# A rebuilt S5 layer with a halved carry pass, weight tiles 320 bytes further on, and stationary values in latent attention

## The chip, the core and the metric

The kernel runs on one core of a Trainium2 chip. The metric is the device time of one execution in microseconds (us), lower being better. The core's engines, each with an instruction queue of its own, are PE (matrix products, TensorE), DVE (VectorE), ACT (ScalarE), POOL (GpSimd) and SP (SyncE, which here issues most DMA transfers). An engine takes its instructions strictly in order: one that waits holds up all behind it.

## What is computed

A network of four layers on 256 positions of 1024 features, all in fp32. The first layer is a state space mixer (S5), the second block attention, the third and fourth are a mixer of three branches (latent attention, convolution, retention) with a feed-forward part. Two pieces matter here.

```python
def s5_mixer(h, w_in, ...):
    u, z = split(h @ w_in)                       # 2 x 1024 columns, u in 64 groups of 16
    # per group and each of 64 complex states: s[t] = a * s[t-1] + f * (b @ u[t])
    _, _, s_re, s_im = lax.associative_scan(_complex_linear_combine, ...)
    y = gelu(c_re @ s_re - c_im @ s_im + d_skip * u)
    y = y * sigmoid(y @ w_glu + b_glu) * silu(z)
    return y @ w_out

def mla_branch(c_q, c_kv, k_pe, ...):            # 8 heads, 96 for scores, 64 for values
    s = q_nope @ k_nope + q_pe @ k_pe
    p = softmax(s * scale)
    return (p @ v) @ w_o
```

## The kernel before

**Products of the later layers.** fp32 products are made of three products of a reduced form: each weight tile is loaded as raw (`wtile`, line 142; DMA L149 on SP), ACT copies its high part hi (L158), DVE subtracts it for the low part lo (L160), and `mm3` (L163) issues L165, L166 and L167. There the activations (xTh, xTl) are the stationary operand, and hi or lo is streamed, 512 columns at a time. `wbuf` (L135) deals out the buffers in turn, in stage 2 (all behind the S5 layer) six of them: of each six tiles four come from the pool wp and two from the pool sp.

```python
        pool, bufs = (self.wp, 4) if i % (4 + more) < 4 else (self.sp, more)
```

Where an sp tile lies follows from the tiles made before it in that pool, one of them the attention mask (`consts2`, L323). By the built program's addresses, the four hi and lo buffers of sp begin at 64 bytes past a multiple of 128 (190016, 194112, 198208, 202304), all those of wp on a multiple of 128. `gemm` (L169) calls `pump` after each tile, which takes one piece of small work from a list (`fill2`); so attention is woven into the weight products.

**The S5 layer** (`s5`, L598). ACT squares x and sums (L625), DVE finds 1/rms (`rsqrt`, L628 and L120 to 133), ACT and DVE scale x (L630, L631), PE turns it (L637), ACT applies the gain (L639). PE then makes u in two halves h of 512 columns (L428, four weight tiles each, two accumulators of two 128-column blocks); `ev_u` stores each block to memory (L649, L650), and four loads per half bring it back regrouped as U (L692). Meanwhile DVE works out the layer's parameters (`s5_params`, `s5_w`, `s5_c`), and PE turns the input matrices into W (L586).

Then for q = 0, 1 PE forms W times U (L729), ACT copies the result into X (L734). X holds 4 chunks g of 16 steps, 32 pairs of groups, real and imaginary. Between q = 0 and q = 1 stands `taps` (L696): products L703, a copy K (L707), the addition of the skip (L708), a store (L709) and 16 loads of M (L716).

DVE scans the 15 steps inside all chunks at once (L743 two products, L745, L747). The carry pass takes g = 1, 2, 3 in turn: powers Q times the carry (L754, four of 128x512), two sums (L756), the next carry (L758) and the additions to X (L762). PE meanwhile makes z (L428) and the part of y inside the chunks (`inside`, L768, L775; `see` copies L779), then waits for X and adds the rest of y (L796, half 0, one z tile, half 1). ACT copies Y (L807), SP stores it (L811) and loads it regrouped (L814), ACT applies gelu (L817), and the gated products follow (L454 to L456).

**Latent attention** (`mla`, L1022) puts 17 pieces into `fill2`. `score(h)`: two products of 256 columns (L1072), DVE's maximum (L1074) and its negative (L1075), two exponentials on ACT with their sums (L1078). `value(h)`: four transposes (L1088), ACT's copy pT (L1090), four products of pT with 64 columns of v streamed (L1097), into a tile with a position per partition. `out(g)` for four heads: reciprocals of the sums, a product of 128x512 on DVE (L1104), four transposes (L1110) and the split into hi and lo.

The order of instructions on an engine is that in which the program issues them, except where small pieces are interleaved with products when it is built, so the built order is read below.

Of the kernel before, what the change touches and what calls it, by code (L numbers as in the profile page):

```python
# [9 lines left out]
F32 = mybir.dt.float32  # L10
# [40 lines left out]
class Net:  # L51
# [267 lines left out]
    def consts2(self):  # L319
# [3 lines left out]
        self.mask = self.sp.tile([128, 128], F32, tag="mask", name="mask", bufs=1)  # L323
# [137 lines left out]
    def s5_params(self):  # L461
# [27 lines left out]
        yield lambda: nc.scalar.activation(cs, r, AF.Sin)  # L489
# [4 lines left out]
        tt(pw[:, 1:3, :, 1], cs, mag[:, None, :].to_broadcast([128, 2, 32]), op=ALU.mult)  # L494
# [4 lines left out]
        def times(out, a, n, re, im):  # L499

            sh = [128, 2, 32, n]
            m = [self.sp.tile(sh, F32, tag="s5m%d" % n, name=self.nm("s5m"), bufs=2) for _ in range(2)]
# [31 lines left out]
        nc.scalar.activation(self.Q[:, :, 0, :], pw[:, :, :, 4], AF.Copy)  # L534
# [54 lines left out]
    def s5_c(self, cab, q, after):  # L589
# [3 lines left out]
        for i in range(2):  # L593
            with self.tc.issue_after(after.ins):
# [3 lines left out]
    def s5(self, x_in):  # L598
# [23 lines left out]
        xr = [self.page([128, 1024], "s5xr") for _ in range(2)]  # L622
        r = self.tmp([128, 2], "pn_r")
        for t in range(2):
            nc.scalar.activation(xr[t], x[t], AF.Square, scale=1.0 / 32, accum_out=r[:, t:t + 1])  # L625
        params = self.s5_params()
        sincos = next(params)
# [5 lines left out]
        for b in range(0, 8, 2):  # L633
            pt = self.small()
            for i in range(2):
                for t in range(2):
                    nc.tensor.transpose(pt[:, i * 256 + t * 128:i * 256 + t * 128 + 128], xr[t][:, (b + i) * 128:(b + i + 1) * 128], self.ident)  # L637
            for i in range(2):
                last = nc.scalar.activation(hT[(b + i) // 4][:, (b + i) % 4], pt[:, i * 256:(i + 1) * 256], AF.Identity, scale=g0[:, b + i:b + i + 1])  # L639
            if b == 0:  # L640
                with self.tc.issue_after(last.ins):
                    sincos()
# [28 lines left out]
        for q in range(4):  # L671
            self.s5_c(cab, q, last)
# [14 lines left out]
        for h in range(2):  # L687
            for go in self.gemm_raw(xs, 512, lambda b, p, h=h: ev_u(4 * h + b, p)):
                go()
            for t in range(4):  # L690
                r = h * 64 + (3 - t) * 16
                self.load_after = nc.sync.dma_start(U[r:r + 16].rearrange("p a g j -> p (a g) j"), uv[h, t])  # L692
# [3 lines left out]
        def taps():  # L696
# [11 lines left out]
            tt(K[:, :, 0:16], K[:, :, 0:16], dk, op=ALU.add)  # L708
            nc.scalar.dma_start(kv[:, :, 48:112], K)  # L709
            M = [self.page([128, 8, 2, 64], "s5M") for _ in range(2)]  # L710
            km = kd.rearrange("(q m c) n -> q c m n", q=2, c=16)
            for q in range(2):
                for t in range(4):
                    r = q * 64 + (3 - t) * 16
                    for h in range(2):
                        nc.sync.dma_start(M[h][r:r + 16].rearrange("p a g n -> p (a g) n"), km[q][:, 16 * h:16 * h + 16, 48 - 16 * t:112 - 16 * t])  # L716
            return M

# [3 lines left out]
        for q in range(2):  # L722
# [12 lines left out]
            if q == 0:  # L735
                M = taps()

        for k in range(1, 16):
# [8 lines left out]
            tt(xo, pr[:, :, :, 0:32], xo, op=ALU.add)  # L747
        for g in range(1, 4):
# [700 lines left out]
```

## Time and profile before

| | us |
|---|---|
| median of 3 runs | 1262.59 (1262.33 to 1263.01) |
| the profiled execution | 1260.24 |
| its span | 1258.5 |
| PE, DVE, ACT busy in the span | 1217.2, 918.9, 663.6 |
| S5 stage: first product, scan, carry pass, Y | 15.00, 59.60, 85.65, 107.25 |

The span is the time from the first to the last record of the profile; 1.74 us of the execution lie around it. Instructions are named by line and engine, operands by the program's tile names with their numbers left out, and "out<-in" gives what is written and read. In a timeline the first number is the start from the beginning of the span, the second the time from the start of the first to the end of the last of the merged instructions, and "x4" their count; a note in brackets is the idle time ahead of them and who ended it. A product of fp32 operands shows as two records, and a record is longer than the distance to the next, since products are pipelined.

### The profile page before, as it was taken

What the parts mean: (1) busy time and instruction counts of PE and PEld (TensorE: products, weight loads), DVE (VectorE), ACT (ScalarE), POOL (GpSimd) and SP (SyncE); (2) the same over time, 40 slices, a digit from 0 to 9 for tenths busy, and PEclk for the clock granted to TensorE, in tenths of its full rate; (3) what the DMA queues carried; (4) which work ended last, traced back from release to release, by engine and by line L of the source; (5) the groups of instructions that cost most, each with busy time, mean ns of one, the idle gap of its engine ahead of it and who ended that gap; (6) DMA issues with size and microseconds to landing.
All of it is one profiled execution on the core that took longest, in us unless ns stands there. A gap on an engine that the chain in (4) does not pass through costs nothing.

```text
span 1258.5 us, 17821 instructions
## 1 busy us (share of the span) xinstructions
PE 1217.2 (97%) x6516; PEld 1013.5 (81%) x6516; DVE 918.9 (73%) x1871; ACT 663.6 (53%) x1107; POOL 3.6 (0%) x16
## 2 busy tenths in 40 slices
PE   6988899999999999999999999999999999999997
PEld 5877787788888888887888887888888887888886
DVE  6793789786899998856655545899997856655544
ACT  5412676766665545546544535666545446544431
POOL 0000000000000000000000000000000000000000
PEclk9998999999999999999999999999999999999999
DMA  8744566542744545563765663644544564765661
GB/s 312 131 68 116 187 195 201 166 142 81 226 136 143 166 144 167 169 213 102 240 193 153 203 231 106 210 137 148 167 150 154 181 200 119 235 185 158 203 208 49
DMA packets 125368, 210.60 MB, mean 167 GB/s; under 512 B 22112, under 2 KB 31328, under 8 KB 125280
## 3 DMA queue, kind: packets, MB, share of 16 engines
q1 hardware_dynamic: 121344, 205.29, 53.7%
q10 hardware_dynamic: 3936, 4.18, 1.1%
q8 instruction: 51, 0.84, 0.3%
q14 instruction: 37, 0.30, 0.1%
HBM read 205.83 MB, written 3.60 MB: 166 GB/s over the span
## 4 chain that ended last, share of the span: by engine, by line
PE 82%; DVE 9%; ACT 3%; DMA 2%; issue 2%; SPq 1%; DVEq 0%; ACTq 0%
PE mm L165 23%; PE mm L167 23%; PE mm L166 23%; PE mm L428 2%; DVE lo L160 2%; PE sm L203 2%; ACT hi L158 1%; PE sm L1097 1%; PE sm L1189 1%; DVE cacc L935 1%; PE sm L1072 1%; DVE s5pr L743 1%; DVE s5fx L754 1%; PE sm L796 1%; PE sm L1177 1%
## 5 line engine op out<-in xcount | busy, mean ns | idle before, releaser
L160 DVE TENSOR_TENSOR lo<-raw,hi 128x1024 fp32r<-128x1024 f32 (+2 forms) x372 | 440.9, 1189 | 230.3 <-ACT hi L158 228.7
L158 ACT ACTIVATE hi<-raw 128x1024 fp32r<-128x1024 f32 (+2 forms) x372 | 382.1, 1032 | 364.9 <-PE mm L167 286.1
L165 PE MATMUL mm<-hi,xTh 128*128 128x512 f32 (+2 forms) x1152 | 451.1, 394 | 1.7 <-ACT xTh L193 1.5
L167 PE MATMUL mm<-hi,xTl 128*128 128x512 f32 (+2 forms) x1152 | 443.7, 386 | 0.3
L166 PE MATMUL mm<-lo,xTh 128*128 128x512 f32 (+2 forms) x1152 | 443.4, 385 | 0.1
L165 PEld LDWEIGHTS mm<-hi,xTh 128*128 128x128 f32 x1152 | 216.4, 188 | 48.9 <-ACT xTh L193 7.2
L167 PEld LDWEIGHTS mm<-hi,xTl 128*128 128x128 f32 x1152 | 216.3, 188 | 46.1 <-DVE t L297 1.5
L166 PEld LDWEIGHTS mm<-lo,xTh 128*128 128x128 f32 x1152 | 216.6, 188 | 41.2 <-DVE lo L160 0.5
L935 DVE SCALAR_TENSOR_TENSOR cacc<-aT,colp,cacc 128x256 f32<-128x256 f32 x240 | 105.4, 488 | 0.0
L165 PE MATMUL mm<-hi,fh 128*128 128x512 f32 x176 | 69.0, 392 | 0.0
L166 PE MATMUL mm<-lo,fh 128*128 128x512 f32 x176 | 68.9, 392 | 0.0
L167 PE MATMUL mm<-hi,fl 128*128 128x512 f32 x176 | 68.8, 391 | 0.0
L167 PEld LDWEIGHTS mm<-hi,fl 128*128 128x128 f32 x176 | 33.0, 187 | 7.3
L165 PEld LDWEIGHTS mm<-hi,fh 128*128 128x128 f32 x176 | 33.0, 188 | 7.3
L166 PEld LDWEIGHTS mm<-lo,fh 128*128 128x128 f32 x176 | 33.0, 188 | 7.2
L277 DVE SCALAR_TENSOR_TENSOR pg<-mm,post 128x512 f32<-128x512 f32 x16 | 11.0, 690 | 21.9 <-ACT pg L275 21.9
L194 DVE SCALAR_TENSOR_TENSOR xTl<-sm,colp,xTh 128x128 fp32r<-128x128 f32 x80 | 24.3, 346 | 3.4 <-ACT xTh L193 3.1
L873 ACT ACTIVATE pg<-mm,t 128x512 f32<-128x512 f32 x24 | 16.5, 689 | 16.9 <-PE mm L167 16.9
L796 PE MATMUL sm<-s5X,s5cab 64*64 64x64 f32 x256 | 14.1, 287 | 11.6 <-DVE s5X L762 11.6
L193 ACT ACTIVATE xTh<-sm,colp 128x128 fp32r<-128x128 f32 x80 | 24.3, 379 | 1.8 <-DVE xTl L194 1.7
L796 PEld LDWEIGHTS sm<-s5X,s5cab 64*64 64x64 f32 x256 | 13.5, 162 | 12.3 <-issue 12.1
L275 ACT ACTIVATE pg<-mm 128x512 f32<-128x512 f32 x16 | 9.5, 596 | 25.9 <-PE mm L167 25.9
(369 smaller groups left out, 1431.8 us busy)
## 6 DMA issues: line engine op xcount, KB each, us to landing
raw<-in_w_in SPq DMA_DIRECT2D x112, 512.0 KB, 3.5
raw<-in_ffn_w_down SPq DMA_DIRECT2D x44, 512.0 KB, 4.2
raw<-in_ffn_w_gate SPq DMA_DIRECT2D x40, 512.0 KB, 4.2
raw<-in_ffn_w_up SPq DMA_DIRECT2D x40, 512.0 KB, 3.7
raw<-in_attn_w_in SPq DMA_DIRECT2D x32, 512.0 KB, 4.4
raw<-in_ret_w_o SPq DMA_DIRECT2D x16, 512.0 KB, 3.3
raw<-in_w_out SPq DMA_DIRECT2D x16, 512.0 KB, 3.3
raw<-in_ssm_w_glu SPq DMA_DIRECT2D x8, 512.0 KB, 5.1
```

Of the source, the lines that this page charges most:

```text
L158: nc.scalar.activation(h, r, AF.Copy)
L160: self.last_lo = nc.vector.tensor_tensor(l, r, h.bitcast(F32), op=ALU.subtract)
L165: nc.tensor.matmul(out, xh, wh, start=first, stop=False)
L166: nc.tensor.matmul(out, xh, wl, start=False, stop=False)
L167: nc.tensor.matmul(out, xl, wh, start=False, stop=last)
L193: a = nc.scalar.activation(dh, src, AF.Copy if isinstance(scale, float) else AF.Identity, scale=scale)
L194: self.last_split = a, nc.vector.scalar_tensor_tensor(dl, src, scale, dh.bitcast(F32), op0=ALU.mult, op1=ALU.subtract)
L203: nc.tensor.transpose(pt[:, b * 128:(b + 1) * 128], row[:, (b0 + b) * 128:(b0 + b + 1) * 128], self.ident)
L428: self.last_raw = nc.tensor.matmul(o, raw[:, k, b * 128:b * 128 + 128], xs[k0 + k], start=k0 + k == 0 and b % 2 == 0, stop=k0 + k == len(x ...
L796: lc = nc.tensor.matmul(pts[g][q * 64:q * 64 + 64, qq * 64:qq * 64 + 64].rearrange("p (g k) -> p g k", g=4), cab[i][pr // 16][r, pr % 16, ...
L873: nc.scalar.activation(gate[t, n], p, AF.Tanh, scale=hf(t))
L935: nc.vector.scalar_tensor_tensor(cacc[:, b, :], src, sc, cacc[:, b, :], op0=ALU.mult, op1=ALU.add)
```

## The change

Three parts.

1. **S5.** PE turns raw x (L634); 1/rms is spread over the partitions by a product of ones with a diagonal (L645, L646, copy L647) and multiplied in by DVE together with the gain (L650). Half 1 of u is made block by block (L708), its U loads are split in two (L717). The taps (L728) come behind all of W times U (L745); the skip is added (L777) and M is loaded behind step 3 of the scan. The carry pass runs over two halves of 16 pairs each (L788 to L798), and after each group ACT copies X into a contiguous Xc (`in_order`, L782), which L835 reads in place of X.
2. **The mask tile** is allocated with 208 floats, of which 128 are used. All later tiles of the pool lie 320 bytes further on; the four hi and lo buffers of sp then begin on a multiple of 128 (190336, 194432, 198528, 202624).
3. **Latent attention.** p is divided by its sum per head (L1120, L1122). The transposes are a piece of their own one round after the score (`turn2`, L1130, copy L1132), and the products (`values`, L1142) keep v stationary and stream 256 positions; two heads fill the two column halves of the result, which is already turned, so that `out` is a split alone. `fill2` gets 18 pieces.

```diff
-        self.mask = self.sp.tile([128, 128], F32, tag="mask", name="mask", bufs=1)
+        self.mask = self.sp.tile([128, 208], F32, tag="mask", name="mask", bufs=1)[:, :128]
...
-        nc.scalar.activation(xr[0], x[0], AF.Identity, scale=r[:, 0:1])
-        nc.vector.tensor_scalar(xr[1], x[1], r[:, 1:2], None, op0=ALU.mult)
+        for t in range(2):
+            dg = self.tmp([128, 128], "s5dg")
+            nc.vector.tensor_scalar(dg, self.ident, r[:, t:t + 1], None, op0=ALU.mult)
+            nc.tensor.matmul(pr_[:, t * 128:t * 128 + 128], ones, dg, start=True, stop=True)
+        nc.scalar.activation(rsb, pr_[:, :256], AF.Copy)
...
+            last = nc.vector.scalar_tensor_tensor(hT[b // 4][:, b % 4], pts[b // 2][:, b % 2 * 256:b % 2 * 256 + 256], g0[:, b:b + 1], rsb,
+                                                  op0=ALU.mult, op1=ALU.mult)
...
+                raws = [self.pre.popleft() for _ in range(4)]
+                for b in range(4):
+                    p = self.acc()[:, :256]
+                    for k in range(8):
+                        self.last_raw = nc.tensor.matmul(p, raws[k // 2][:, k % 2, b * 128:b * 128 + 128], xs[k], start=k == 0, stop=k == 7)
+                    ev_u(4 + b, p)
...
-            if q == 0:
-                M = taps()
-
+        K = taps()
...
+            if k == 3:
+                with self.tc.issue_after(ls.ins):
+                    tt(K[:, :, 0:16], K[:, :, 0:16], dk, op=ALU.add)
+                spread()
+
+        def in_order(h, g):
+            for i in range(2):
+                self.last_xc = nc.scalar.activation(Xc[i][h][:, :, 16 * g:16 * g + 16], X[:, g, 0:16, i, 16 * h:16 * h + 16].rearrange("p k a -> p a k"), AF.Copy)
+        for h in range(2):
+            s = slice(16 * h, 16 * h + 16)
+            in_order(h, 0)
+            for g in range(1, 4):
+                if g == 1:
+                    nc.vector.tensor_copy(X[:, 1, 0, :, s], X[:, 0, 16, :, s])
+                pr = self.page([128, 2, 2, 16, 16], "s5fx")
                 for i in range(2):
-                    tt(pr[o][:, i], self.Q[:, 1 - o + i], X[:, g, 0, i, None, :].to_broadcast([128, 16, 32]), op=ALU.mult)
+                    for o in range(2):
+                        tt(pr[:, i, o], self.Q[:, 1 - o + i, :, s], X[:, g, 0, i, None, s].to_broadcast([128, 16, 16]), op=ALU.mult)
+                tt(pr[:, 0], pr[:, 0], pr[:, 1], op=ALU.add)
...
+                in_order(h, g)
+            if h == 0:
+                lxc = self.last_xc
+        self.split_after = lxc, ls
...
-                                      cab[i][pr // 16][r, pr % 16, 1:5].rearrange("p l c -> p (l c)"), X[r, :, 0:16, i, pr],
+                                      cab[i][pr // 16][r, pr % 16, 1:5].rearrange("p l c -> p (l c)"), Xc[i][h][r, pr % 16],
...
+            ri = self.tmp([128, 2], "m_ri")
+            nc.vector.reciprocal(ri, rsum[:, :, h])
+            for t in range(2):
+                nc.scalar.activation(pr[:, t, :], pr[:, t, :], AF.Identity, scale=ri[:, t:t + 1])
...
+            for kb in range(2):
+                for hh in range(2):
+                    h = 2 * b + hh
+                    nc.tensor.matmul(po[g][hh * 64:hh * 64 + 64, (b % 2) * 256:(b % 2) * 256 + 256], vr[:, kb, h, :], pTs[h][:, kb, :],
+                                     start=kb == 0, stop=kb == 1, skip_group_check=True)
...
-            rinv = self.tmp([128, 2, 4], "m_ri")
-            nc.vector.reciprocal(rinv, rsum[:, :, 4 * g:4 * g + 4])
-            o = self.tmp([128, 2, 4, 64], "m_o")
-            nc.vector.tensor_tensor(o, po[g].rearrange("p (t h d) -> p t h d", t=2, h=4),
-                                    rinv[:, :, :, None].to_broadcast([128, 2, 4, 64]), op=ALU.mult)
...
-            self.split(oT[0][0][:, s, :], oT[0][1][:, s, :], pt.rearrange("p (b n) -> p b n", b=2))
+            self.split(oT[0][0][:, s, :], oT[0][1][:, s, :], po[g].rearrange("p (b n) -> p b n", b=2))
```

Where the order moves, first ACT's queue at the end of the carry pass, before (X has been copied by L734 long before; L779 are the small copies, L158 the hi parts of w_glu, L807 is Y):

```order
L779 ACTIVATE t_148_952<-sm_918 128x8
L779 ACTIVATE t_149_954<-sm_919 128x8
L158 ACTIVATE hi_1113<-raw_1112 128x1024
L779 ACTIVATE t_152_998<-sm_964 128x8
L779 ACTIVATE t_153_1000<-sm_965 128x8
L158 ACTIVATE hi_1119<-raw_1118 128x1024
L158 ACTIVATE hi_1125<-raw_1124 128x1024
L807 ACTIVATE s5Y_888<-sm_918 128x8x64
```

and in the change, from the last group of half 0 on (775 and 777 are Xc of half 0, 776 and 778 of half 1; L818 are the small copies, L846 is Y):

```order
L782 ACTIVATE s5Xc_775<-s5X 128x16x16
L782 ACTIVATE s5Xc_777<-s5X 128x16x16
L158 ACTIVATE hi_1161<-raw_1160 128x1024
L782 ACTIVATE s5Xc_776<-s5X 128x16x16
L782 ACTIVATE s5Xc_778<-s5X 128x16x16
...
L818 ACTIVATE t_157_1008<-sm_974 128x8
L818 ACTIVATE t_158_1010<-sm_975 128x8
L158 ACTIVATE hi_1167<-raw_1166 128x1024
L818 ACTIVATE t_161_1058<-sm_1024 128x8
L818 ACTIVATE t_162_1060<-sm_1025 128x8
L158 ACTIVATE hi_1173<-raw_1172 128x1024
L846 ACTIVATE s5Y_936<-sm_974 128x8x64
```

Y of half 0 now stands behind the copies of half 1 (three pairs, of which one is shown), the small copies and two hi parts.

Second, PE's queue in latent attention, before (two transposes and values of neighbouring heads around a score):

```order
L1088 MATMUL sm_4115<-first,pg_4071 128x128 x4
L1097 MATMUL sm_3999<-mv_3596,pg_4079 128x64 x4
L1072 MATMUL sm_4147<-mkT_3692,mqT_3690 128x256 x2
L1097 MATMUL sm_3999<-mv_3596,pg_4120 128x64 x4
L1088 MATMUL sm_4156<-first,pg_4112 128x128 x4
```

and in the change, heads 4 to 7 (L1111 is the score, L1130 the turn; 4322 is p of head 6, whose score is 4316; 4262 and 4334 are the turned p of heads 4 and 5):

```order
L1111 MATMUL sm_4316<-mkT_3740,mqT_3738 128x256 x2
L1130 MATMUL sm_4329<-first,pg_4250 128x128 x4
...
L1111 MATMUL sm_4357<-mkT_3740,mqT_3738 128x256 x2
L1130 MATMUL sm_4370<-first,pg_4322 128x128 x4
L1142 MATMUL sm_4377<-pg_4262,mv_3644 64x256
L1142 MATMUL sm_4377<-pg_4334,mv_3644 64x256
L1142 MATMUL sm_4377<-pg_4262,mv_3644 64x256
L1142 MATMUL sm_4377<-pg_4334,mv_3644 64x256
```

The values of two heads now stand together, their column halves in turn, and where rows are left out twelve weight products stand.

## Rows read from the trace of the kernel before

**Rows 1.** The page: busy time by engine, the last chain, the largest products.
```profile
PE 1217.2 (97%) x6516; PEld 1013.5 (81%) x6516; DVE 918.9 (73%) x1871; ACT 663.6 (53%) x1107; POOL 3.6 (0%) x16
...
PE 82%; DVE 9%; ACT 3%; DMA 2%; issue 2%; SPq 1%; DVEq 0%; ACTq 0%
...
L165 PE MATMUL mm<-hi,xTh 128*128 128x512 f32 (+2 forms) x1152 | 451.1, 394 | 1.7 <-ACT xTh L193 1.5
...
L165 PE MATMUL mm<-hi,fh 128*128 128x512 f32 x176 | 69.0, 392 | 0.0
```
**Rows 2.** Busy time by stretch: window, length, then busy us of each engine.
```profile
85.00:100.00 15.00, 3.36 (x102) 3.25 (x97) 14.93 (x30) 3.44 (x7) 0.00 (x0) 0.78 0.00 1
```
**Rows 3.** The timeline of PE through the S5 stage.
```profile
15.00 3.62 PE L428 MATMUL mm<-s5x,raw 128*128 128x256 f32 x16
...
46.44 3.95 PE L729 MATMUL sm<-s5U,s5W 64*64 64x64 f32 x128
50.32 0.76 PE L703 MATMUL sm<-s5cab,s5Bd 128*32 128x64 f32 x39
52.15 1.47 PE L703 MATMUL sm<-s5cab,s5Bd 128*32 128x64 f32 x89 [1.07 <-issue]
...
55.59 2.89 PE L729 MATMUL sm<-s5U,s5W 64*64 64x64 f32 x90 [0.66 <-issue]
...
99.97 7.24 PE L796 MATMUL sm<-s5X,s5cab 64*64 64x64 f32 x128 [11.64 <-DVE s5X L762]
```
**Rows 4.** The timeline of ACT through the S5 stage.
```profile
10.40 1.15 ACT L630 ACTIVATE s5xr<-x,t 128x1024 f32<-128x1024 f32 x1 [1.93 <-DVE t L133]
...
56.66 2.91 ACT L734 ACTIVATE s5X<-sm 128x512 f32<-128x512 f32 x3 [0.51 <-PE sm L729]
...
88.38 0.24 ACT L779 ACTIVATE t<-sm 128x8 f32<-128x8 f32 x2 [0.88 <-PE sm L775]
88.50 2.00 ACT L158 ACTIVATE hi<-raw 128x1024 fp32r<-128x1024 f32 x2
107.25 1.08 ACT L807 ACTIVATE s5Y<-sm 128x512 f32<-128x512 f32 x2 [16.74 <-PE sm L796]
```
**Rows 5.** The timeline of DVE through the S5 stage.
```profile
49.70 1.43 DVE L553 TENSOR_TENSOR s5q<-s5Q 128x256 f32<-128x256 f32 x4
...
59.60 0.76 DVE L743 TENSOR_TENSOR s5pr<-s5a,s5X 128x256 f32<-128x256 f32 x2 [4.97 <-ACT s5X L734]
...
85.65 2.50 DVE L754 TENSOR_TENSOR s5fx<-s5Q,s5X 128x512 f32<-128x512 f32 x4
...
99.17 1.23 DVE L762 TENSOR_TENSOR s5X<-s5fx,s5X 128x480 f32<-128x480 f32 x2
```
**Rows 6.** The timeline of PE in a run of weight products, 601 to 618 us.
```profile
603.30 0.39 PE L165 MATMUL mm<-hi,xTh 128*128 128x512 f32 x1
...
612.14 0.39 PE L165 MATMUL mm<-hi,xTh 128*128 128x512 f32 x1
...
614.70 0.39 PE L167 MATMUL mm<-hi,xTl 128*128 128x512 f32 x1
```
**Rows 7.** Latent attention: the timeline from 369 us, and whom L1097 waited for.
```profile
371.01 1.03 PE L1072 MATMUL sm<-mkT,mqT 96*128 96x256 f32 x4
...
374.38 0.47 ACT L1078 ACTIVATE pg<-sm,t 128x256 f32<-128x256 f32 x1
374.73 0.20 ACT L1078 ACTIVATION_READ_ACCUMULATOR pg<-sm,t 128x1 f32 x1
375.48 0.60 PE L1088 MATMUL sm<-first,pg 128*128 128x128 f32 x4
379.90 1.10 PE L1097 MATMUL sm<-mv,pg 128*128 128x64 f32 x8 [0.78 <-ACT pg L1090]
...
  ACT pg L1090: 2.9, 5
```

More of the change, by code (lines that the diff above doesn't have):

```diff
@@ L628, in s5 @@
+        for b in range(0, 8, 2):
+            pts.append(self.small())
+            for i in range(2):
+                for t in range(2):
+                    nc.tensor.transpose(pts[-1][:, i * 256 + t * 128:i * 256 + t * 128 + 128], x[t][:, (b + i) * 128:(b + i + 1) * 128], self.ident)
+        params = self.s5_params(sq)
+        next(params)
         nc.vector.tensor_scalar(r, r, EPS, None, op0=ALU.add)
         self.rsqrt(r, r)
-        nc.scalar.activation(xr[0], x[0], AF.Identity, scale=r[:, 0:1])
@@ L631, in s5 @@
-        nc.vector.tensor_scalar(xr[1], x[1], r[:, 1:2], None, op0=ALU.mult)
-        g0 = self.g0
[L633 to L642, printed above, removed]
+        ones = self.sp.tile([128, 128], F32, tag="s5one", name="s5one", bufs=1)
@@ new lines, in s5 @@
+        nc.gpsimd.memset(ones, 1.0)
+        rsb = self.sp.tile([128, 256], F32, tag="s5rsb", name="s5rsb", bufs=1)
+        pr_ = self.acc()
+        for t in range(2):
[3 more added lines that the diff above has]
+        nc.scalar.activation(rsb, pr_[:, :256], AF.Copy)
+        g0 = self.g0
+        for b in range(8):
+            last = nc.vector.scalar_tensor_tensor(hT[b // 4][:, b % 4], pts[b // 2][:, b % 2 * 256:b % 2 * 256 + 256], g0[:, b:b + 1], rsb,
+                                                  op0=ALU.mult, op1=ALU.mult)
+            if b == 1:
+                self.two = last
@@ L687, in s5 @@
         for h in range(2):
[L688 to L692, printed above, removed]
+            if h == 0:
+                for go in self.gemm_raw(xs, 512, lambda b, p: ev_u(b, p)):
+                    go()
+            else:
+                raws = [self.pre.popleft() for _ in range(4)]
[4 more added lines that the diff above has]
+                    ev_u(4 + b, p)
+                while self.todo and len(self.pre) < 12:
+                    self.load_raw()
+            for e in range(1 + h):
+                a = slice(8 * e, 8 * e + 8) if h else slice(0, 16)
+                for t in range(4):
+                    r = h * 64 + (3 - t) * 16
+                    self.load_after = nc.sync.dma_start(U[r:r + 16, a].rearrange("p a g j -> p (a g) j"), uv[h, t][:, 2 * a.start:2 * a.stop])
         Wl = [[self.page([128, 8, 128], "s5W") for _ in range(2)] for _ in range(2)]
@@ L707, in taps @@
             nc.scalar.activation(K, pt.rearrange("p (a n) -> p a n", a=8), AF.Copy)
[L708 to L717, printed above, removed]
+            return K
         X = s5p.tile([128, 4 * 17 * 64], F32, tag="s5X", name="s5X").rearrange("p (g s r a) -> p g s r a", g=4, s=17, r=2)
@@ L783, in s5 @@
             zg += self.gemm_raw(xs, 512, lambda b, p, h=h: ev_z(4 * h + b, p))
-        for i in range(7):
+        for i in range(6):
             zg.popleft()(lx)
-        self.drain(self.fill2)
+        zg.popleft()()
         gT = self.pages(8, "s5g")
@@ L1115, in mla @@
         f += [lambda t=t, g=g: turn(t, g) for g in range(2) for t in range(2)]
-        f.append(lambda: score(0))
-        for h in range(8):
-            if h < 7:
-                f.append(lambda h=h: (score(h + 1), value(h)))
-            else:
-                f.append(lambda h=h: value(h))
-            if h % 4 == 3:
-                f.append(lambda g=h // 4: out(g))
+        f += [lambda: score(0), lambda: (score(1), turn2(0)), lambda: (score(2), turn2(1))]
+        for h in range(2, 8):
+            f.append(lambda h=h: (score(h + 1) if h < 7 else None, turn2(h), values(h // 2 - 1) if h % 2 == 0 else None))
+            if h == 4:
+                f.append(lambda: out(0))
+        f += [lambda: values(3), lambda: out(1)]
         return oT
```

86 lines of the change are left out of this document (41 added, 45 removed).

## The prediction

> **What bounds the kernel now.** I read the page first. PE is busy for 97% of the span, and the chain that ended last runs 82% over PE and 9% over DVE [rows 1]. So for most of the span a microsecond taken from PE's queue is a microsecond of the result, and work on DVE and ACT costs nothing while it stays behind PE. Then I read busy time by stretch: the exception is 85 to 100 us, where PE works 3.36 of 15 us and DVE 14.93 [rows 2]. Last I read the timelines of PE, ACT and DVE through the S5 stage [rows 3 to 5], PE's stream of weight products [rows 6] and the latent attention [rows 7].
>
> The S5 stage is a serial chain. PE forms the inputs U and the products L729; ACT copies them into X, the last copy ending at 56.66 + 2.91 = 59.57 [rows 4]; DVE scans from 59.60 and then runs the carry pass until 99.17 + 1.23 = 100.40 [rows 5]; PE waits 11.64 us, starts L796 at 99.97 and needs 7.24 us for its first half [rows 3]; ACT takes Y at 107.25 [rows 4]. From Y on there are stores, loads, gelu and the gated products, and the change keeps their order.
>
> The profiled execution took 1260.24 us, 2.35 under the median of 1262.59; the sum is made against the former and carried over to the median unchanged.
>
> **Part 1, the S5 layer.**
> Start: before, ACT normalises x from 10.40 to 11.55, PE turns it, and the first product starts at 15.00 [rows 3, 4]. In the change PE turns raw x while the norm is still being worked out. Of the path behind the norm there remain a diagonal on DVE, two products of 128 columns, one ACT copy and one DVE product of 128x256, four of which take 1.43 [rows 5]; I put these at 2.0 us from 10.4, so the first product comes at 12.5: 2.5 us earlier. The bounds are 0 (the new work is as long as the old) and 4.
> Products: the second half of W_in is done block by block. That is the same 64 products, so everything up to L729 keeps its 46.44 - 15.00 = 31.4 us [rows 3], and L729's successor starts at 43.9. U's second half is now stored and loaded some 3 us earlier, in eight loads instead of four, on SP's queue ahead of nothing urgent. Before, L729 is cut in two: 128 records in 3.88 us, then the taps L703, with waits of 1.07 and 0.66, then the rest until 55.59 + 2.89 = 58.48 [rows 3]. In the change the 256 records run in one piece: 7.8 us, to 51.7. The last copy into X ended 1.1 us behind the last product before; I allow 1.2, so the scan starts at 52.9, 6.7 us earlier. The taps come behind the products, where PE would otherwise go on with the z tiles; their sums are needed only when M is loaded, some 25 us later, so I cost them at nothing. If that cover is gone, M's 16 loads make L814 late; there PE still has seven z tiles to do first, each like the first product's 16 records of 3.62 us [rows 3], 25 us.
> Scan: 15 steps from 59.60 to the carry pass's first work at 85.65 [rows 5], 26 us, plus 0.3 for the one addition put in behind step 3: it ends at 79.2.
> Carry pass: before 85.65 to 100.40. A half's group is four products of 256 elements (1.43 for four), one sum of 512 (0.62, a quarter of 2.50) and an addition of 480 (0.61, half of 1.23) [rows 5], with 0.1 for the next start: 2.75 us. Three groups and two small copies make 8.5 a half, 17 for both: DVE needs 2.3 us more, to 96.2. But the first half stands at 87.7, so PE's first half of L835 (7.2 us, as L796 took) runs under DVE's second half.
> Y: here ACT's order decides. Y's first copies stand in the queue behind the last pair of the new copies Xc (I put it at 0.8, between 0.24 for two of 8 columns and 2.00 for two of 1024), four small copies L818 (as L779, 0.24 for two) and two of L158 (2.00) [rows 4]. That is 3.2 us behind DVE's end: Y at 99.4 instead of 107.25. **Part 1 gives -8.** Were Y not queued so, it would come at 95.6 and the part give 11.6; if the pieces ahead of the scan gain only the start, it gives 3. These are its ends.
>
> **Part 2, the mask tile of 208 floats.** It computes nothing, but moves every later tile of that pool by 320 bytes, among them the four hi and lo buffers that hold the fifth and sixth of each six weight tiles. In PE's stream of 512 columns, products start 227 ns apart in four tiles of six, then 233 ns in two. In the rows: 39 starts from 603.30 to 612.14, 8.84 us or 226.7 each; then 11 from 612.14 to 614.70, 2.56 us or 232.7 [rows 6]. This change of pace recurs with the same six-fold period through the span, and by the program's addresses the slow tiles begin 64 bytes past a multiple of 128 and the others on one; moved, they all begin on one. The weight is the streamed operand here. The two largest sets of products are 3 x (1152 + 176) = 3984 records [rows 1]; a third, 1328, times 6.0 ns is **-8 us**. I take all of it, since PE is the bound where these run; the narrower forms among them I leave at nothing, within 0.5. The other end is 0: period and address go together here, but what else may be peculiar to these buffers the trace cannot part.
> The Trainium skill, in TensorE: Matmul & The Clock Gate, Part 2, "Step-by-step: what each phase is for", says that throughput is purely N cycles, measured there as 215.7 ns for 512 columns, with no word on the address. By it this part would be worth 0 and the sum -14; the trace shows two paces for one shape at the same granted clock, and neither is 216.
>
> **Part 3, the values of latent attention, two layers of eight heads.**
> Products: before, a head's four products L1097 are eight records in 1.10 us, of which the last 0.27 is its own length; about 0.9 a head, 14 for 16 heads [rows 7]. In the change a head has two products of 256 columns. A score L1072 has that width: four records in 1.03, with 0.38 for the last, 0.217 apart, so two instructions take 0.87 [rows 7], 13.9 for 16 heads if they run one after another. But neighbours write different halves of the columns, as in L729, where 128 records start 31 ns apart, 62 an instruction [rows 3], against 0.87/2/4 = 109 for 64 columns by the score's row. By that ratio the 13.9 become 7.9: -6. Ends: 0 and -7.
> Transposes: 16 of the 128x128 kind go with out(); four in 0.60 with 0.27 for the last [rows 7] are 0.11 each: -1.8.
> Waits: L1097's 2.9 us of waiting for ACT's pT copy [rows 7] go, as the turn now stands ahead of the values by a round or more.
> New waits: a turn now needs a reciprocal on DVE and two more ACT passes of 0.47. Before, p stood 2.9 us behind the score's end (372.04 to 374.93) [rows 7]; now 4.1 to 5.3, by how busy DVE is. PE's queue leaves 12 to 17 weight products and a little small work between score and turn for five heads of eight, 3.6 to 5 us, and far more for the other three. I take 0.4 us for each of ten heads: +4. Ends: 0 and 1.5 each, +15. Behind a waiting turn the next weight products queue.
> ACT gets 32 passes of 0.47, 15 us in two stages where it idles half the time: nothing, as long as hi stays ahead of PE. **Part 3 gives -6**, ends -12 and +6.
>
> Sum: -8 - 8 - 6 = -22, 1238.2 for a profiled execution, **1240.6** as a median.
>
> **The rivals.**
> *The address decides nothing.* Part 2 is 0: 1248.6. For it speaks the rule above, and that a buffer's place and its turn cannot be parted here; against it that the pace changes at the very product that begins such a tile, with weights, shapes and neighbours all alike.
> *The scan does not start earlier than the norm allows.* If ACT's copies into X or U's loads replace the waits that went, only the start is gained: part 1 gives 3, 1245.6. For it: ACT's copies of 0.97 each (2.91 for three) already pace L729 nearly as PE does. Against it: eight of them are 7.8 us, as long as the products.
> *Slower: the turns wait in ACT's queue.* ACT works in order, and a head's two passes stand behind hi copies that can themselves wait for a load. If each of the 16 turns waits on average over (22 + 4 + 2.5)/16 = 1.8 us, the change ends slower; 2.6 each would cost 42 in place of 4 and give 1279. Against it: before, PE waited at no turn, and half of the heads have long distances.
> *No effect anywhere* would need all three parts to fail; each touches a different stage.
>
> **How the numbers follow.** All parts as forecast, within their ends: 0.70, by itself 1233 to 1248. Address without effect: 0.13. Scan held back: 0.12. Slower by the turns: 0.03; in between, 0.02. Parts 1 and 3 both near their good ends give 1231, part 2 at nothing with the others a little short 1251; the range 1231 to 1251 leaves out under 2 in 10. A measurement can tell about 0.2%, 2.5 us, from no change: faster 0.95, same 0.02, slower 0.03.
>
> **What would show it.** The first product at 12.5, the scan at 52.9, Y near 99.4 with ACT at work on L158 just ahead of it; products 227 ns apart in all six tiles; the values as groups with starts near 0.12, and waits at L1130 of 4 us in all. The forecast is wrong if the slow tiles keep 233, if Y follows 20 us or more behind the first half, or if PE shows waits above 1 us at most turns.

## The result and the profile after

The changed kernel takes **1249.32 us**, median of 4 runs (1248.01 to 1251.77), beside 1262.80 for the kernel before (1262.33 to 1266.08): a ratio of 0.9886 with a 95% interval of 0.9867 to 0.9905, 13.5 us faster. The forecast was 1240.6, 22 us faster, with a range of 1231 to 1251. The sign and the range hold; 8.5 us of the gain did not come. The profiled execution of after took 1251.77 us (span 1249.0), only 8.5 less than that of before: the S5 stage does not run alike in every execution of one kernel, as the experiments show. So the traces are read here stage by stage, and sizes are taken from the runs' ratios and medians.

The page of the kernel after, as [rows 1]:

```profile
PE 1208.6 (97%) x6440; PEld 1005.0 (80%) x6440; DVE 921.0 (74%) x1901; ACT 682.1 (55%) x1147; POOL 3.8 (0%) x17
...
PE 82%; DVE 9%; ACT 4%; issue 2%; DMA 2%; SPq 1%; DVEq 0%; ACTq 0%
...
L165 PE MATMUL mm<-hi,xTh 128*128 128x512 f32 (+2 forms) x1152 | 449.8, 393 | 1.7 <-ACT xTh L193 1.5
...
L165 PE MATMUL mm<-hi,fh 128*128 128x512 f32 x176 | 68.7, 390 | 0.0
```

PE is busy 8.6 us less (1217.2 to 1208.6), ACT 18.5 us more, and the chain still runs 82% over PE. Both groups of weight products are a little shorter than in [rows 1].

The timeline of PE through the S5 stage after, as [rows 3]:

```profile
10.69 0.68 PE L646 MATMUL mm<-pg,s5one 128*128 128x128 f32 x4 [1.32 <-DVE pg L645]
12.37 5.41 PE L428 MATMUL mm<-s5x,raw 128*128 128x256 f32 x16 [0.99 <-DVE s5x L650]
...
45.37 3.95 PE L745 MATMUL sm<-s5U,s5W 64*64 64x64 f32 x128
50.48 6.86 PE L745 MATMUL sm<-s5U,s5W 64*64 64x64 f32 x128 [1.17 <-ACT s5X L750]
...
85.30 5.04 PE L814 MATMUL sm<-s5U,s5M 64*64 64x64 f32 x128
102.66 5.04 PE L835 MATMUL sm<-s5Xc,s5cab 64*64 64x64 f32 x128 [12.32 <-ACT t L818]
```

The timeline of ACT there, as [rows 4]:

```profile
93.55 1.18 ACT L782 ACTIVATE s5Xc<-s5X 128x256 f32<-128x256 f32 x2 [1.45 <-DVE s5X L798]
...
101.36 1.18 ACT L782 ACTIVATE s5Xc<-s5X 128x256 f32<-128x256 f32 x2 [1.54 <-DVE s5X L798]
102.44 0.22 ACT L818 ACTIVATE t<-sm 128x8 f32<-128x8 f32 x2
...
107.73 1.09 ACT L846 ACTIVATE s5Y<-sm 128x512 f32<-128x512 f32 x2 [3.04 <-PE sm L835]
```

And of DVE, as [rows 5]:

```profile
58.46 0.76 DVE L770 TENSOR_TENSOR s5pr<-s5a,s5X 128x256 f32<-128x256 f32 x2 [6.72 <-ACT s5X L750]
...
84.31 0.27 DVE L788 COPY s5X<-s5X 128x32 f32<-128x32 f32 x2
...
92.87 0.65 DVE L798 TENSOR_TENSOR s5X<-s5fx,s5X 128x480 f32<-128x480 f32 x1
...
100.67 0.66 DVE L798 TENSOR_TENSOR s5X<-s5fx,s5X 128x480 f32<-128x480 f32 x1
```

The stage between 85 and 100 us, as [rows 2] (window, length, then busy us of PE, weight loads, DVE, ACT and POOL, the granted clock of PE, DMA share, GB/s):

```profile
85.00:100.00 15.00, 5.33 (x130) 4.90 (x128) 14.69 (x38) 8.07 (x13) 0.00 (x0) 0.84 0.01 1
```

DVE still fills this stretch (14.69 of 15 us), and of PE little more than L814 stands in it. The scan starts at 58.46 instead of 59.60, the carry pass runs from 84.31 to 100.67 + 0.66 = 101.33, and Y comes at 107.73: in this execution the rebuilt layer gains nothing on Y against the profiled execution of before (107.25 in [rows 4]). PE was through with L814 at 85.30 + 5.04 = 90.34. Then it stood for 12.32 us, 0.7 longer than it had stood for L796 [rows 3], and its row says for whom: ACT's L818. The carry pass's first half was through at 92.87 + 0.65 = 93.52 and copied into Xc by 93.55 + 1.18 = 94.73. But the two copies L818 of eight columns stand in ACT's queue behind the copies L782 of the second half too, the last pair from 101.36, and run at 102.44. So PE's **first** half of L835 starts when the **second** half of the carry pass is through. That is the largest thing that the forecast missed.

Weight products after, as [rows 6], and latent attention, as [rows 7]:

```profile
598.07 0.39 PE L165 MATMUL mm<-hi,xTh 128*128 128x512 f32 x1
...
611.90 0.40 PE L167 MATMUL mm<-hi,xTl 128*128 128x512 f32 x1
```

From 598.07 to 611.90 there are 61 starts: 13.83 us, 226.7 ns each, with no stretch at 233. Before, the pace changed after 39 [rows 6]. In the whole trace some 3900 weight products of 512 columns are followed at once by another; 1735 of these distances were 230 to 236 ns in before, 553 are in after. Those that are left in a stretch that I went through (600 to 640 us) stand right behind small products.

Groups of instructions by line, then the timeline of PE in the first of the two latent attentions:

```profile
L1142 PE MATMUL sm<-pg,mv 128*64 128x256 f32 x64 | 11.2, 395 | 0.0
L1130 PE MATMUL sm<-first,pg 128*128 128x128 f32 x64 | 11.2, 276 | 0.2 <-ACT pg L1122 0.2
```

```profile
391.91 0.65 PE L1142 MATMUL sm<-pg,mv 128*64 128x256 f32 x2
392.49 0.55 PE L1130 MATMUL sm<-first,pg 128*128 128x128 f32 x3
392.96 1.08 PE L1142 MATMUL sm<-pg,mv 128*64 128x256 f32 x6
393.97 1.13 PE L1111 MATMUL sm<-mkT,mqT 96*128 96x256 f32 x4
...
409.66 1.08 PE L1142 MATMUL sm<-pg,mv 128*64 128x256 f32 x8
410.67 0.50 PE L165 MATMUL mm<-hi,xTh 128*128 128x512 f32 x1
```

At L1130 PE waits 0.2 us once in both layers (0.6 once in e0_again). Gone are L1097's waits for pT. But of the 2.9 us in [rows 7] PE itself stood only 0.8, once, the 0.78 shown there; the other 2.1 are idle time of its weight loads (PEld), which overlap PE.

### The profile page after: what moved, and what is told of

Its sections match the earlier page's. It is cut to its first block, busy times and chain, and to the rows that moved or that the text cites. A ratio compares the mean times of both kernels' runs of the same rounds, so it can differ in the third digit from the quotient of the medians.

```text
span 1249.0 us, 17728 instructions
## 1 busy us (share of the span) xinstructions
PE 1208.6 (97%) x6440; PEld 1005.0 (80%) x6440; DVE 921.0 (74%) x1901; ACT 682.1 (55%) x1147; POOL 3.8 (0%) x17
## 4 chain that ended last, share of the span: by engine, by line
PE 82%; DVE 9%; ACT 4%; issue 2%; DMA 2%; SPq 1%; DVEq 0%; ACTq 0%
PE mm L165 23%; PE mm L167 23%; PE mm L166 23%; PE sm L203 2%; DVE lo L160 2%; PE mm L428 1%; ACT hi L158 1%; PE sm L1222 1%; PE mm L708 1%; PE sm L1111 1%; DVE cacc L974 1%; DVE s5pr L770 1%; PE sm L1142 1%; DVE s5fx L792 1%; PE sm L745 1%
## 5 line engine op out<-in xcount | busy, mean ns | idle before, releaser
L158 ACT ACTIVATE hi<-raw 128x1024 fp32r<-128x1024 f32 (+2 forms) x372 | 382.5, 1032 | 351.0 <-PE mm L167 294.0
L454 PE MATMUL mm<-s5gh,hi 128*128 128x256 f32 x64 | 19.1, 304 | 4.8 <-ACT s5gh L861 3.2
L1400 ACT ACTIVATE pg<-mm,t 128x512 f32<-128x512 f32 (+1 forms) x24 | 15.6, 652 | 13.9 <-PE mm L167 13.9
```

Of the source, the lines that this page charges most:

```text
L158: nc.scalar.activation(h, r, AF.Copy)
L454: nc.tensor.matmul(o, wh, xh, start=first and b % 2 == 0, stop=False, skip_group_check=True)
L1400: nc.scalar.activation(sg[t][:, :nn], p, AF.Silu, scale=rstd[:, t:t + 1])
```

## The experiments

All ratios are to the kernel before on the same chip, with 95% intervals; the gains of the single parts are worked out from the ratios. The kernel before had medians of 1263.82, 1263.93 and 1262.97 us in the three groups of runs (e0 to e3, e4 to e7, e8 and e9).

### The three parts, each alone

**e0_again** is the changed kernel unaltered, once more.

> The changed kernel once more. Theory 1: in the first profile TensorE ran from 51 to 61 us at half clock after the wait of 1.17 us at 49.3, which cost 2.9 us in L745 and 1.6 in L728, and that profiled execution (1251.77) was the slowest of four; if the drop is a matter of chance, a second profile shows L745's second half at 4 us instead of 6.86 and an execution near 1248.5. Rival: the drop belongs to this program, and every profile shows it; then 6.86 us again, and the spread of the times comes from elsewhere.

Measured: 1248.01 us, ratio 0.9880 (0.9867 to 0.9893), 15.8 us under its neighbours. So the two comparisons put the whole at -13.5 and -15.8 by medians, -14.4 and -15.2 by ratios. The execution is near the 1248.5 of theory 1, but the second half of L745 took 6.17 us, not 4: the low clock came again.

**e1_mask** is the kernel before with the one line of the mask:

```diff
-        self.mask = self.sp.tile([128, 128], F32, tag="mask", name="mask", bufs=1)
+        self.mask = self.sp.tile([128, 208], F32, tag="mask", name="mask", bufs=1)[:, :128]
```

> The kernel before with the mask tile of 208 floats alone. Theory 1: it gives what the paces show, 1328 products by 6 ns, so -8 us, 1254.5 to 1255. Rival: a product that starts 6 ns earlier meets its next wait 6 ns earlier; the stages where PE waits for weights give it back, and -4 or less is left.

Measured: 1257.60 us, 0.9957 (0.9943 to 0.9971): **-5.4 us**, between 3.7 and 7.2, so between theory and rival. Nothing but addresses moves, so the rival of a part 2 without effect falls. The opposite proof is e3_s5, which has the rebuilt layer but not this line. Its weight products, in the same place of the program:

```profile
602.22 0.39 PE L165 MATMUL mm<-hi,xTh 128*128 128x512 f32 x1
...
611.06 0.39 PE L165 MATMUL mm<-hi,xTh 128*128 128x512 f32 x1
...
613.63 0.39 PE L167 MATMUL mm<-hi,xTl 128*128 128x512 f32 x1
```

39 starts in 8.84 us, 226.7 each, then 11 in 2.57, 233.6: the step of [rows 6] is still there. Pace and address go together in the five runs where I compared both: the two kernels of the diff, e0_again, e1_mask and e3_s5. Only one shift, 320 bytes, was tried; that the multiple of 128 is what counts is not shown.

Why 5.4 and not 8? The products themselves gave the 8: over the 3760 distances up to 240 ns the mean falls from 229.74 ns in before to 227.59 in e1_mask, 8.1 us in all. Part of it is given back where a faster PE meets the next engine sooner. The latent attention of e1_mask, timeline of PE:

```profile
384.46 1.10 PE L1097 MATMUL sm<-mv,pg 128*128 128x64 f32 x8 [1.40 <-ACT pg L1090]
...
387.03 0.63 PE L165 MATMUL mm<-hi,xTh 128*128 128x512 f32 x1
387.45 0.63 PE L166 MATMUL mm<-lo,xTh 128*128 128x512 f32 x1
```

The wait for ACT's pT copy is 1.40 here where it was 0.78 [rows 7], and behind it five products from 386.17 start 0.42 us apart instead of 0.23; the granted clock was 0.57 in the stretch from 386 to 390. That is some 2 us in this place and this execution. Matched product by product, e1_mask gains 4.3 us on before from the first weight product behind the S5 layer to the last; the second latent attention gives back another 0.6, and the rest was not followed.

The profiled execution of e1_mask took 1260.24 us all the same, as much as that of before, for its S5 layer, the same code, ran longer. PE and ACT in it:

```profile
57.20 4.17 PE L729 MATMUL sm<-s5U,s5W 64*64 64x64 f32 x90 [0.94 <-issue]
...
110.06 1.09 ACT L807 ACTIVATE s5Y<-sm 128x512 f32<-128x512 f32 x2 [14.73 <-PE sm L796]
```

The same 90 records took 2.89 us in before [rows 3], and Y came at 107.25 [rows 4]. The scan started at 62.48 (62.33 in e2_values, which has this layer at the old addresses) for 59.60, and the first weight product at 151.52 (151.33) for 147.24. So the execution that the forecast was made from had a short S5 stage, and one execution beside another can't size part 1.

**e2_values** is the kernel before with the latent attention of the change (the last hunk of the diff); **e3_s5** the kernel before with the S5 layer of the change (all other hunks but the mask's).

> The kernel before with the latent attention of the change alone. Theory 1: the alignment of the two traces moves by -2.5 and -2.2 us across the two attention stages, of which some 0.7 each belong to the weight tiles, so -3.5 us, 1259. Rival: the forecast -6, hidden in the sum because another part lost; then 1256.5.

> The kernel before with the S5 layer of the change alone. Theory 1: L835 waits for the small copies L818, which stand in ACT's queue behind all copies of half 1, so that halving the carry pass gives nothing: Y at 107 to 108 as before and a total within 2 us of the kernel before. Rival: the profiled run was an unlucky one, and the part gives its -8 in others: 1254.5, Y near 99.

Measured: e2_values 1259.64 us, 0.9966 (0.9953 to 0.9980): **-4.3 us**, nearer to its theory than to its rival. e3_s5 1259.11, 0.9968 (0.9957 to 0.9979): **-4.0 us**, more than its theory allowed and half of its rival's; in its trace L835 does wait for L818, 13.15 us, but the scan starts at 55.39 and Y comes at 105.02. The three parts add up to 5.4 + 4.3 + 4.0 = 13.7 us, which is the whole within its error. So by the medians they hardly get in each other's way, as far as an error of 1.5 us for each can tell, and each fell short by itself: of the 22 forecast part 1 lacks 4.0 us, part 2 2.6 and part 3 1.7.

### What holds Y back

**e4_see** puts the copies into Xc of the second half behind the small copies L818 (now L820), and **e5_y** moreover puts Y's first copies ahead of the last two groups of them and of the hi parts:

```diff
+            if h == 0:
+                in_order(h, g)
...
+                self.see = nc.scalar.activation(self.tmp([128, 8], "s5see"), yp[h][g].rearrange("p (q j) -> p q j", j=64)[:, :, 63], AF.Copy)
...
+        for g in range(4):
+            with self.tc.issue_after(self.see.ins):
+                in_order(1, g)
```

In e5_y the last loop is `range(2)`, and in the loop over L840, behind Y's copies:

```diff
+            if h == 0:
+                for g in range(2, 4):
+                    with self.tc.issue_after(ly.ins):
+                        in_order(1, g)
+                self.split_after = ly, ls
```

> The change with the small copies (L818 there) put ahead of the copies Xc of half 1 in ACT's queue; nothing else moves. Theory 1: L835 waited for these copies alone, so it starts near 91 instead of 102 us and its half 0 is done by 96; Y then waits for ACT, which has Xc of half 1 until 102.5 and one hi part before it, so Y near 103.5 instead of 107.5: 4 us less than the change, 1244 to 1245. Rival: L835 waits for something else of half 1 and starts near 102 again; no gain.

> As the one before, and Y's first copies besides ahead of the last two groups of Xc of half 1 and of the hi parts of w_glu. Theory 1: Y follows the end of L835's half 0, near 97, and what comes behind moves with it: 10 us less than the change, 1238 to 1240. Rival: the tail behind Y is bound by something else (stores on SP, w_glu's loads, the table load), and half of it or less arrives: 1243 or more.

Measured: e4_see **1245.39 us**, 0.9850 (0.9835 to 0.9865), near its theory; e5_y **1241.41**, 0.9828 (0.9814 to 0.9842), between theory and rival, the fastest of all, some 22 us under the kernel before and 6.6 under e0_again. In e4_see, the timeline of PE:

```profile
92.96 5.38 PE L840 MATMUL sm<-s5Xc,s5cab 64*64 64x64 f32 x128 [7.33 <-ACT t L820]
```

and ACT:

```profile
92.74 0.23 ACT L820 ACTIVATE t<-sm 128x8 f32<-128x8 f32 x2
...
93.92 3.42 ACT L782 ACTIVATE s5Xc<-s5X 128x256 f32<-128x256 f32 x6
...
100.58 1.07 ACT L851 ACTIVATE s5Y<-sm 128x512 f32<-128x512 f32 x2
```

L820 runs at 92.74 instead of 102.44, L840 (which was L835) starts right behind it, and PE's half now runs under DVE's second half, as forecast. It ends at 92.96 + 5.38 = 98.34, but Y, at 100.58, stands behind more copies and a hi part. In e5_y, ACT:

```profile
91.60 0.36 ACT L820 ACTIVATE t<-sm 128x8 f32<-128x8 f32 x4
91.83 2.32 ACT L782 ACTIVATE s5Xc<-s5X 128x256 f32<-128x256 f32 x4
97.68 1.09 ACT L844 ACTIVATE s5Y<-sm 128x512 f32<-128x512 f32 x2 [3.53 <-PE sm L840]
98.65 2.25 ACT L782 ACTIVATE s5Xc<-s5X 128x256 f32<-128x256 f32 x4
```

Y comes at 97.68 and now waits for PE alone, 10 us ahead of the change's 107.73. The gelu of the second half, the last link of the stage, comes at 119.62 instead of 128.24, 8.6 ahead; of these the median shows 6.6. That the copies L818 held PE, and not DVE or the products, is so shown: nothing else was moved in e4_see. Leaving the copies L818 out altogether was not tried.

### When the scan can start

**e6_u** gives U's second half back its old form (both halves with `gemm_raw`, four loads instead of eight); **e7_taps** puts the taps back between the two halves of L745.

```diff
-            if h == 0:
...
+            for go in self.gemm_raw(xs, 512, lambda b, p, h=h: ev_u(4 * h + b, p)):
+                go()
+            for t in range(4):
+                r = h * 64 + (3 - t) * 16
+                self.load_after = nc.sync.dma_start(U[r:r + 16].rearrange("p a g j -> p (a g) j"), uv[h, t])
```

```diff
-        K = taps()
+            if q == 0:
+                K = taps()
```

> The change with u's second half as before: both accumulators at once, four loads of U. Theory 1: the blocks that finish early wait for a free buffer and for SP, so doing them one by one gives nothing, and the total stays within 1.5 us of the change (1247 to 1250), the scan's start within 1 us of 57.4 to 58.5. Rival: U's second half would come 3 us later still, the scan starts at 60 or later, but as L835 waits for ACT anyway the total moves by 2 to 3 us: 1251.

> The change with the taps back between the halves q = 0 and q = 1 of the products of W and U. Theory 1: the products of q = 1 wait for U's second half (1.3 us) whether the taps stand there or not, so the taps fill that wait, PE keeps its full clock and the second half takes 4 us instead of 6.2 to 6.9; the scan starts no later than in the change, and the total is 0 to 2 us less: 1246 to 1248.5. Rival: as forecast, the taps ahead of q = 1 put the scan 1.5 to 2 us later, and the total is 1250 or more.

Measured: e6_u 1254.34 us, 0.9923 (0.9910 to 0.9935), 5 to 6 us slower than the change, so its theory is wrong. Its second half of L745, timeline of PE:

```profile
52.84 7.09 PE L732 MATMUL sm<-s5U,s5W 64*64 64x64 f32 x128 [3.57 <-DMA s5U<-s5ud]
```

It waits 3.57 us for U's load and begins 2.4 us later than in the change, and the scan follows at 61.05. So block by block is worth doing, and the wait shows what rules here: the landing of U. e7_taps: 1250.67 us, 0.9904 (0.9889 to 0.9919). Its interval overlaps those of the change, so its 1.4 to 2.7 us are not told apart from nothing, but the gain of its theory did not come.

In the change, SP's queue at that place:

```profile
30.35 6.44 SPq L661 DMA_DIRECT2D s5ud<-pg  x3
38.33 1.91 SPq L717 DMA_DIRECT2D s5U<-s5ud  x4
40.28 2.48 SPq L661 DMA_DIRECT2D s5ud<-pg  x3
45.12 4.66 SPq L717 DMA_DIRECT2D s5U<-s5ud  x8
```

The last three stores L661 of U's second half stand behind the loads of its first half, which go out at 38.33, when the first half's stores have landed (the page gives a store a median of 5.7 us for that). So these stores go out from 40.28 on and the second loads from 45.12, the last issue ending at 45.12 + 4.66 = 49.78. Before, the four loads were issued between 46.02 and 47.93. They now start 0.9 us earlier, not 3, and end 1.9 later.

**e8_busy** is e5_y with twelve more transposes, whose output nobody reads, where PE stands still ahead of the first products; **e9_both** moreover has five instead of four buffers for the small tiles.

```diff
+        for _ in range(6):
+            nc.tensor.transpose(pr_[:, 256:384], x[1][:, 896:1024], self.ident)
...
+        for _ in range(6):
+            with self.tc.issue_after(lm.ins):
+                nc.tensor.transpose(pd[:, :128], x[1][:, 896:1024], self.ident)
```

```diff
-    net.stage(15, 4)
+    net.stage(15, 5)
```

> The version with Y ahead in ACT's queue, and twelve transposes more whose result nobody reads, six behind the transposes of x and six behind the products with the diagonal, so that PE does not stop before the first product of u. Theory 1: the first weight tile took 5.2 to 6.3 us in place of 3.5 because PE ran at half clock after those two waits; now it takes 3.5 to 4. But the loads of U's second half were issued at 45.1 in every run of the changed layer, however early PE was, so the scan still starts at 55 or later and the total does not fall: within 2 us of 1241.4. Rival: PE's products bind; the scan starts 2.5 us earlier, near 53, and the total is 1238.5 to 1239.5.

> The same with one more buffer (five instead of four) for small tiles in the S5 stage, so that the copy of u's fifth block no longer waits 4 to 5 us for the first blocks' stores to land. Theory 1: that copy comes near 32 instead of 36 us, the stores and with them the first four of the eight loads of U's second half are issued 2 to 4 us earlier, and the scan starts at 53 to 54; 1239 to 1240. Rival: the stores land late because the weight loads fill the DMA engines until about 43 us; the loads stay at 45, and the total is that of the run without the buffer.

Measured: e8_busy 1242.52 us, 0.9839 (0.9826 to 0.9853); e9_both 1244.04, 0.9847 (0.9833 to 0.9862): neither is faster than e5_y. That is what e8_busy's theory said; that of e9_both, 1239 to 1240, is wrong. The timeline of PE in e8_busy, and the same places in e5_y:

```profile
12.29 3.72 PE L428 MATMUL mm<-s5x,raw 128*128 128x256 f32 x16 [0.34 <-DVE s5x L656]
...
44.47 3.95 PE L751 MATMUL sm<-s5U,s5W 64*64 64x64 f32 x128 [0.80 <-DMA s5U<-s5ud]
49.70 5.70 PE L751 MATMUL sm<-s5U,s5W 64*64 64x64 f32 x128 [1.28 <-DMA s5U<-s5ud]
```

```profile
12.64 6.29 PE L428 MATMUL mm<-s5x,raw 128*128 128x256 f32 x16 [0.99 <-DVE s5x L650]
...
46.52 7.78 PE L745 MATMUL sm<-s5U,s5W 64*64 64x64 f32 x256
```

Here PE does its first tile in 3.72 us instead of 6.29 and is 2 us earlier at L751. That the twelve transposes did it is not shown: e0_again has none and took 3.72 too. At L751 PE waits for U, 0.80 and 1.28 us, and its second half then takes 5.70 instead of 3.9. The stretches of 51 to 61 us, e8_busy and e5_y (columns as above; the granted clock is the 0.66 and the 1.00):

```profile
51.00:61.00 10.00, 10.00 (x230) 9.54 (x227) 4.81 (x13) 4.73 (x5) 0.00 (x0) 0.66 0.16 52
```

```profile
51.00:61.00 10.00, 9.34 (x251) 8.50 (x248) 6.22 (x16) 4.99 (x6) 0.00 (x0) 1.00 0.22 61
```

So the scan of e8_busy starts at 56.53, 1.1 us later than the 55.42 of e5_y. In e9_both the extra buffer lets ACT's fifth copy go at 31.02 instead of 35.67, yet the second loads go out no earlier:

```profile
45.56 4.87 SPq L723 DMA_DIRECT2D s5U<-s5ud  x8
```

In all runs of the changed layer these loads begin between 44.38 and 45.56, whatever PE's pace. A buffer is not what they wait for. By the trace's landing times it is one store, the first of the three that stand behind the first half's loads: in the eight runs with split loads it goes out between 39.59 and 40.47, right behind those loads, lands 4.6 to 5.1 us later, and the second loads go out 0.01 to 0.02 us after that. In e9_both its data was copied by 36.63, and it still went out at 40.47. Putting that store ahead of the first loads was not tried.

Leaving out e6_u and e7_taps, whose order ahead of the scan is another, the runs with the new layer sort by this. In e3_s5, e4_see and e5_y the first tile took 6.1 to 6.3 us, L745 ran in one piece at full clock and the scan started between 55.39 and 55.62. In the change, e0_again, e8_busy and e9_both the first tile took 5.41 or 3.72, L745 waited 1.2 to 2.2 us for what it needed, the clock from 51 to 61 us was 0.50 to 0.66, and the scan started between 56.53 and 59.04. **Where PE came earlier, the scan came later.** In the change itself the row names ACT's copy as what the second half waited for, in the others U's load; at 50.48 against 49.94 and 49.70 it may be either. That the wait brings the lower clock is the order of events in these traces and not shown by itself: e7_taps has a gap of 1.01 us in its second half and keeps 1.00, and so does the kernel before with gaps of 1.07 and 0.66 [rows 3]. Nor is it the new layer's alone: e1_mask, with gaps of 1.07 and 0.94 in the old one, has 0.87 from 51 to 61 us and the 4.17 us for 90 records shown above.

## Why the prediction was right, and where it was not

The number lies in the range, near its slow end, and in part by luck. The sum leaned on an execution with a short S5 stage: beside its 147.24 the first weight product comes at 147.83 in the change, 145.45 in e0_again and 145.97 in e3_s5, so beside that execution part 1 gives at most 1.8 us. And in part 3 errors of opposite sign met.

**Part 1, forecast -8, alone -4.0.** Right: the first product (12.37 for 12.5), the length of the scan (58.46 to 84.31 is 25.9 for 26.3), the carry pass (84.31 to 101.33 is 17.0 for 17), and L818 named as standing in ACT's queue.

- *Failed: "U's second half is now stored and loaded some 3 us earlier, ... ahead of nothing urgent", and with it the scan at 52.9.* I moved loads along with the products that feed them, but they wait for stores behind other loads. L745's second half never began before 49.70; in e5_y, which had no wait, it began near 50.4 (46.52 and half of 7.78), and its 3.9 us and the copy behind it put the scan at 55.4. In the change it came at 58.46, 5.6 late: 2.7 for a second half that began at 50.48 where the forecast has 47.8, and 2.9 for its 6.86 us at half clock. The earlier start gave nothing for the same reason; 1.8 of it went again in the first tile (5.41 for 3.62), behind waits of 1.32 and 0.99 us, though e0_again had such waits and took 3.72. The rival "the scan does not start earlier than the norm allows" named U's loads and gave part 1 three; with 0.12 of the chance it is near to what happened in this half of the part.
- *Failed: "PE's first half of L835 runs under DVE's second half".* I counted L818 only in the queue ahead of Y. But L835 adds into the tiles that L818 reads, so PE waits for L818 and L818 for every copy into Xc ahead of it. Y came 107.73 - 101.33 = 6.4 us behind DVE instead of 3.2: L835's 5.04, and the copies. e4_see and e5_y show the forecast's own picture once the order is mended.

**Part 2, forecast -8, alone -5.4.** The pace is confirmed as forecast: 233 falls to 227 where nothing but the address moves, and stays where it doesn't; the products' own 8.1 us are the term. The step that was mis-sized is "I take all of it, since PE is the bound where these run": where PE comes earlier it also meets ACT earlier. The wait of 1.40 in e1_mask and the half clock behind it are the largest such place that was found, some 2 us in its one trace; of the 2.6 that its median lacks the trace can't tell the shares. In the change L1097 and this wait are gone: from the first weight product to the last it gains 10.4 us on before and e0_again 10.0, where e1_mask gains 4.3 and e2_values 4.2. The rule of the Trainium skill that stood against this part (TensorE: Matmul & The Clock Gate, Part 2, "Step-by-step: what each phase is for": N cycles and nothing else) is contradicted by e1_mask and e3_s5, 226.7 and 233.6 ns for the same 512 columns.

**Part 3, forecast -6, alone -4.3.** Its terms were off in both directions (as written they add up to -6.7). *Failed: "L1097's 2.9 us of waiting for ACT's pT copy ... go".* PE stood 0.8 of them; 2.1 were its weight loads'. New waits: 0.2 us at L1130 instead of 4, so the rival of turns waiting in ACT's queue falls. Products: 64 of them from start to next start sum to 10.4 us in the change against 13.6 for the 128 of L1097, -3.2 instead of -6; a block of eight records takes 1.30 on average. The ratio taken from L729 was right for a block in one piece: 409.66 to 410.67 is 1.01 us for eight records, 0.13 each against 7.9/64 = 0.12. But some blocks are cut by other work: the one at 391.91 has a turn between its second and third record, and takes 0.58 until the turn (391.91 to 392.49) and 1.01 for the six records behind it (392.96 to 393.97), 1.59 in all. From such a product to a full-width one it is 309 ns from start to start, where a product of 256 columns has 217. The Trainium skill states in TensorEngine Tiling (Array Packing), "Key Properties", that changing the tiling mode drains the engine; the trace agrees, with the 309 beside it. Transposes: 1.4 us gone for 1.8 forecast. Not in the forecast: the 64 transposes that stay sum to 6.7 us instead of 6.0 (+0.7), the scores to 12.7 instead of 13.1 (-0.4). With the 0.8 and the 0.2 that makes -4.9, beside 4.3 measured (2.5 to 5.9).

**Sum.** Short by 4.0, 2.6 and 1.7 us, 8.3 together, which is the missing 8.5 within the error of the runs.

## What to carry to other kernels

When work is split so that one engine can start on the first half, follow every operand of the first consumer, the accumulators that it adds into among them, and ask what stands ahead of their releaser in its own in-order queue; here two copies of eight columns, queued behind the second half, held PE for 12 us, and mending the order there and at Y was worth 6.6 us, more than part 1 gave without it. A transfer that is issued earlier lands earlier only if what its own queue waits for is earlier too. Speeding up the producer ahead of a fixed landing time is no gain. And before a stage is sized from one execution, see how much that stage differs between executions of the same code: here by 4 us, as much as the part gave.

## What the runs showed that I had not expected

- A streamed weight tile that begins 64 bytes past a multiple of 128 costs 233 ns a product of 512 columns, one on a multiple 227, at the same granted clock (1.00 in both stretches of [rows 6]).
- In five profiled executions of nine with the new layer the small products from 51 to 61 us ran with a granted clock of 0.50 to 0.66, so mostly at the level of 1.2 GHz; in the other four it was 1.00. The scan started between 56.53 and 61.05 in the five and between 55.39 and 57.30 in the four; how much of that is the clock's is not shown.
- In latent attention two products L1142 in different column halves start 6 to 8 ns apart; the next pair comes 209 ns later (260 behind a block's first pair).
- L835 reads contiguous copies and writes without a rearranged pattern: its second 128 products take 3.78 us, those of L796 6.90, both at a granted clock of 1.00. I had given it L796's time. Which of the two changes does it was not tried.
